# Order of heads in the small matmuls of a recurrent branch, halves of a product, and a stacked low-rank pass

## The chip, the cores and the metric

The kernel runs on one core of one Trainium2 chip. The metric is the device time of one execution in microseconds; the median of three runs stands for the kernel.

## What is computed

One layer of a hybrid model over 2048 positions and 1024 channels, in float32: an input projection, a gated MLP branch with a spatial product in chunks of 128, a recurrent branch of eight heads, a gated merge of both, an output projection with residual and layer norm, and a feed-forward layer of 4096 with residual and layer norm. The change touches the recurrent branch:

```python
r, k, v, xw, xa, xg = jnp.split(z, [i1, i2, i3, i4, i5], axis=-1)
w_log = -jax.nn.softplus(-(w0 + jnp.tanh(xw) @ w_decay_up)) - 0.5
decay = jnp.exp(-jnp.exp(w_log.astype(jnp.float32)))
a = jax.nn.sigmoid(a0 + xa @ w_aaa_up)
...
def step(state, inp):
    rt, wt, kt, vt, at, bt = inp
    sa = jnp.einsum('bhij,bhj->bhi', state, at)
    state = (state * wt[:, :, None, :] + sa[..., None] * bt[:, :, None, :]
             + vt[..., None] * kt[:, :, None, :])
    yt = jnp.einsum('bhij,bhj->bhi', state, rt)
    return state, yt
```

The two products with `w_decay_up` and `w_aaa_up` contract over 32 values each; they are called the low-rank products below. Heads have 64 channels.

## The kernel before

The sequence is cut into four blocks of 512 positions. The large products (projections, gates, merge, output, feed-forward) are run as three float32r matmuls each, on a high and a low part of both operands (`mm3`, lines 453 to 455), with 512 columns. Weights come from DRAM as tiles of 128 x 1024 (`wraw`); ScalarE casts the high part `whi` (line 387), VectorE subtracts to the low part `wlo` (line 388), one tile ahead of their use.

The recurrent branch is computed in chunks of 64 positions. A block has four half-blocks of 128 positions (two chunks), and the eight heads are four pairs; of a pair the even head lies in partitions 0 to 63 (`half[0]`, `E`), the odd one in 64 to 127 (`half[1]`, `O`). Each half-block passes three stages, all in plain f32:

- `rwkv_a`, for each pair: the low-rank products into `ua` (lines 587, 588), decays and scaled operands on ScalarE and VectorE, then the score products `s0` and `s1` (line 625; even head on the upper rows of the array, odd head on the lower), a sum over a head (626) and transposes (628). The operand `xwa` is computed per block in `proj_rwkv`, goes out to DRAM (`xd`) and comes back per half-block, into two sets of buffers.
- `rwkv_b`: the inverse of a triangular matrix per head and chunk. VectorE makes the 32 x 32 diagonal blocks in 31 steps (lines 687, 688), they pass through DRAM (`td`, `TT`), are transposed on VectorE into `T11` (line 708), and 32 x 32 matmuls make the off-diagonal block (lines 712 and 719), first all of the even heads, then all of the odd ones.
- `rwkv_c`, for each of two chunks: Q's product `xy` (line 759) of the state with the chunk's operands, with all 128 weights columns of `G`, so that one product gives both the value that the inverse is applied to (copied to `Xs`) and the first part of the output; the product with the inverse, `TT` (line 768); the state update (774); the second part of the output, added in place (780). Each runs over the four pairs of the even heads, then over those of the odd ones. Copies out of PSUM are split between VectorE and ScalarE by head.

TensorE's instructions stand in the order in which the program is written; the other engines' order is chosen by a scheduler when the program is built. The large products are generators that yield after every two k-tiles (six matmuls), and `weave` takes a step of the recurrent branch whenever the step before has had its number of yields (`Y_C` is 2, `Y_T` 12, and so on). So between two small groups lies a fixed number of large matmuls. Block 0's recurrent branch runs beside the projections of blocks 0 and 1, that of each later block beside the feed-forward and projections around it. The very first products (`first`, from `first_tiles` in `setup`) run before any of this.

Of the kernel before, what the change touches and what calls it, by code (L numbers as in the profile page):

```python
# [16 lines left out]
P = 128  # L17
# [3 lines left out]
TB = 512  # L21
# [68 lines left out]
class Body:  # L90
# [122 lines left out]
    def setup(self):  # L213
# [69 lines left out]
        self.lora = const.tile([C, 2, RW], F32, name="lora")  # L283
        nc.sync.dma_start(out=self.lora, in_=A["lora"])
# [226 lines left out]
    def proj_rwkv(self, b):  # L511
        nc, A = self.nc, self.A
        if self.h_of != b:
            self.go(self.load_h(b))
        xwa = self.work.tile([C, TB], F32, name="xwa", tag="t2", bufs=3)
        pp = self.pre[0] if b == 0 else (yield from self.fm(self.hT, m=C))
        self.shift_mix(pp, C, "xwa", 0, 12, xwa)
        nc.scalar.activation(xwa[0:32], xwa[0:32], AF.Tanh)
        xg = self.work.tile([96, TB], F32, name="xg", tag="t2", bufs=3)
        pp = self.pre[1] if b == 0 else (yield from self.fm(self.hT, m=96))  # L520
        self.shift_mix(pp, 96, "xg", 0, 13, xg)
        nc.scalar.activation(xg, xg, AF.Tanh, scale=0.5)
        nc.vector.tensor_scalar(xg, xg, 0.5, 0.5, op0=ALU.mult, op1=ALU.add)
        xd = self.dr.tile([TB // HB, C + 96, HB], F32, name="xd", tag="xd", bufs=2)
        nc.sync.dma_start(out=xd[:, 0:C].rearrange("h p t -> p h t"), in_=xwa.rearrange("p (h t) -> p h t", t=HB))
        nc.sync.dma_start(out=xd[:, C:].rearrange("h p t -> p h t"), in_=xg.rearrange("p (h t) -> p h t", t=HB))
        zd = [self.dr.tile([TB // HB, P, 3, HB], F32, name=f"zd{p}", tag=f"zd{p}", bufs=2) for p in range(NP)]
        self.spill["z", b] = (xd, zd)
# [25 lines left out]
    def rwkv_a(self, b, h, q):  # L554
# [13 lines left out]
        xd, zd = self.spill["z", b]  # L568
        xwa = rp.tile([C, HB], F32, name="xwa", tag="xwa", bufs=2)
        nc.sync.dma_start(out=xwa, in_=xd[h, 0:C])  # L570
        xg = rp.tile([96, HB], F32, name="xg", tag="xg", bufs=2)
        nc.sync.dma_start(out=xg, in_=xd[h, C:])
# [8 lines left out]
        def first(p):  # L581
# [5 lines left out]
            nc.tensor.matmul(ua[:, 0], lhsT=self.lora[:, 0, fs], rhs=xwa, start=True, stop=True)  # L587
            nc.tensor.matmul(ua[:, 1], lhsT=self.lora[:, 1, fs], rhs=xwa, start=True, stop=True)
# [31 lines left out]
        def second(p, bk, kp):  # L620
            zr, zk, zv = (zq[:, p, j] for j in range(3))
            s0, s1 = pst([P, 3, P], "s0"), pst([P, 4, P], "s1")
            for i, sc in enumerate((s0, s1)):
                for c in range(NC):
                    nc.tensor.matmul(sc[:, c], lhsT=bk[half[i], c], rhs=G[i][half[i], p, c], start=True, stop=True)  # L625
# [38 lines left out]
    def rwkv_b(self, q):  # L664
# [52 lines left out]
        for i, (lo, hi) in enumerate(qd):  # L717
            for u in range(U16):
                nc.tensor.matmul(tps[lo, u], lhsT=Zs[hi, u], rhs=TT[hi, u, 32:64], start=True, stop=True)
# [5 lines left out]
    def rwkv_c(self, b, h, q):  # L725
# [20 lines left out]
        for c in range(NC):  # L746
# [14 lines left out]
            Xs = rp.tile([P, NP, C], F32, name="Xs", tag="Xs", bufs=1)  # L761
            nc.vector.tensor_copy(out=Xs[E], in_=xy[E, 0])
            nc.scalar.copy(out=Xs[O], in_=xy[O, 1])
            yield Y_C
            for i in range(2):
                r = half[i]
                for p in range(NP):
# [4 lines left out]
            for i in range(2):  # L772
                for p in range(NP):
# [4 lines left out]
            for i in range(2):  # L778
                for p in range(NP):
                    nc.tensor.matmul(xy[half[1 - i], i, p], lhsT=AB[half[i], p, c, cr[i]:cr[i] + C], rhs=Q[half[i], i, p],  # L780
                                     start=False, stop=True, skip_group_check=True)
            nc.vector.tensor_mul(self.Sc[self.scur], St, PC[:, c][:, :, None].to_broadcast([P, NP, C]))
            nc.scalar.copy(out=Yt[half[c], :, 0], in_=xy[O, 0])
            nc.vector.tensor_copy(out=Yt[half[c], :, 1], in_=xy[E, 1])
# [303 lines left out]
def arrange(np, inp):  # L1088
# [37 lines left out]
    lora = np.zeros((64, 2, 512), w.dtype)  # L1126
    lora[:32, 0] = inp["w_decay_up"][0]
    lora[32:, 1] = inp["w_aaa_up"][0]
    a["lora"] = lora
# [44 lines left out]
```

## Time and profile before

| | |
|---|---|
| median of 3 runs | 3103.5 us (3100.29 to 3109.51) |
| the profiled execution | 3111.15 us |
| its span, first to last instruction | 3109.3 us |
| TensorE busy | 3046.7 us (98%) |
| VectorE busy | 2124.0 us (68%) |
| ScalarE busy | 1263.4 us (41%) |

The page of the profile gives busy times over the whole span. Matmuls are pipelined, so they overlap in the records, and how long a stretch of TensorE takes is read from the starts in the timeline. In the timeline, equal instructions that follow each other stand in one row with their count, and the time of the row goes from the first start to the last end. A f32 matmul leaves two matmul records, a float32r one leaves one. PE is TensorE, DVE is VectorE, ACT is ScalarE.

### The profile page before, as it was taken

The page shows a single profiled execution, that of the slowest core. Times are in us where ns is not written, and L with a number is a line of the kernel's source. Part 1 is how long each engine was busy: PE and PEld are TensorE (multiplying, and loading weights), DVE is VectorE, ACT ScalarE, POOL GpSimd, SP SyncE. Part 2 cuts the span into 40 slices and gives each one's busy share as a digit, 9 for nine tenths or more (in the row PEclk, how much of TensorE's full clock was granted, in tenths as well). Part 3 has the DMA queues.
Part 4 walks back from the last instruction along what each step waited for, and adds up shares of the span by engine and source line. Part 5 has one row for each costly group of instructions (what it writes and reads, how often), then busy time and mean ns, then how long its engine had stood idle before and what let it go on. Part 6 is the DMA issues. An engine that isn't in the chain of part 4 may idle for free.

```text
span 3109.3 us, 44483 instructions
## 1 busy us (share of the span) xinstructions
PE 3046.7 (98%) x16432; PEld 2455.4 (79%) x16432; DVE 2124.0 (68%) x4727; ACT 1263.4 (41%) x2012; POOL 149.2 (5%) x370
## 2 busy tenths in 40 slices
PE   8999999999999999999999999999999999999998
PEld 6776878777777877878787888787878888888887
DVE  7877874778777686486777657567668755854446
ACT  5534433353343334444433343453444334253332
POOL 1101100000000000100000000110000000000000
PEclk9999999999999999999999999999999999999999
DMA  8565544832323265433323246534333224622332
GB/s 286 158 177 165 169 135 161 271 102 86 98 82 102 82 204 190 152 129 120 104 92 93 89 142 205 164 121 148 118 97 93 84 95 146 223 88 95 98 99 95
DMA packets 241483, 416.71 MB, mean 134 GB/s; under 512 B 72465, under 2 KB 127377, under 8 KB 241265
## 3 DMA queue, kind: packets, MB, share of 16 engines
q1 hardware_dynamic: 241184, 413.59, 41.7%
q8 instruction: 130, 2.13, 0.3%
q14 instruction: 89, 0.72, 0.1%
q0 software_dynamic: 80, 0.26, 0.0%
HBM read 357.60 MB, written 56.17 MB: 133 GB/s over the span
## 4 chain that ended last, share of the span: by engine, by line
PE 85%; DVE 9%; DMA 4%; issue 1%; ACT 1%; SPq 0%; POOL 0%; DVEq 0%; ACTq 0%
PE fm_ps L453 15%; PE fm_ps L455 14%; PE fm_ps L454 14%; PE ff L453 7%; PE ff L454 7%; PE ff L455 7%; PE xy L759 2%; DVE wlo L388 1%; PE ops L454 1%; PE ops L455 1%; PE ops L453 1%; DVE tmp L687 1%; PE s L625 1%; PE vps L453 1%; PE us L768 1%
## 5 line engine op out<-in xcount | busy, mean ns | idle before, releaser
L387 ACT CAST whi<-wraw 128x1024 fp32r<-128x1024 f32 (+1 forms) x500 | 495.0, 991 | 880.7 <-PE fm_ps L454 439.5
L388 DVE TENSOR_TENSOR wlo<-wraw,whi 128x1024 fp32r<-128x1024 f32 (+1 forms) x500 | 573.0, 1148 | 343.2 <-ACT whi L387 335.7
L453 PE MATMUL fm_ps<-xh,whi 128*128 128x512 f32 x1984 | 796.1, 401 | 3.6 <-ACT xh L387 2.2
L454 PE MATMUL fm_ps<-xl,whi 128*128 128x512 f32 x1984 | 774.4, 390 | 2.8 <-DVE xl L388 2.8
L455 PE MATMUL fm_ps<-xh,wlo 128*128 128x512 f32 x1984 | 775.7, 391 | 0.6 <-DVE wlo L388 0.6
L453 PEld LDWEIGHTS fm_ps<-xh,whi 128*128 128x128 f32 x1984 | 370.8, 187 | 91.9 <-issue 5.2
L455 PEld LDWEIGHTS fm_ps<-xh,wlo 128*128 128x128 f32 x1984 | 370.8, 187 | 84.0 <-DVE wlo L388 1.5
L454 PEld LDWEIGHTS fm_ps<-xl,whi 128*128 128x128 f32 x1984 | 371.4, 187 | 77.4 <-DVE xl L388 4.3
L453 PE MATMUL ff<-hh,whi 128*128 128x512 f32 (+1 forms) x1056 | 416.2, 394 | 1.9 <-DVE zr L1051 1.2
L454 PE MATMUL ff<-hl,whi 128*128 128x512 f32 (+1 forms) x1056 | 404.8, 383 | 0.3 <-DVE hl L388 0.3
L455 PE MATMUL ff<-hh,wlo 128*128 128x512 f32 (+1 forms) x1056 | 405.1, 384 | 0.0
L1051 DVE SCALAR_TENSOR_TENSOR zr<-ff,mod,zr 128x512 f32<-128x512 f32 (+1 forms) x264 | 184.9, 730 | 138.6 <-PE ff L455 138.1
L453 PEld LDWEIGHTS ff<-hh,whi 128*128 128x128 f32 x1056 | 198.6, 188 | 46.2 <-issue 6.0
L455 PEld LDWEIGHTS ff<-hh,wlo 128*128 128x128 f32 x1056 | 198.4, 188 | 40.3
L454 PEld LDWEIGHTS ff<-hl,whi 128*128 128x128 f32 x1056 | 198.8, 188 | 35.6 <-DVE hl L388 0.5
L687 DVE TENSOR_TENSOR tmp<-T,L 128x4 f32<-128x4 f32 (+23 forms) x496 | 162.3, 327 | 10.2
L688 DVE TENSOR_REDUCE T<-tmp 128x1 f32<-128x4 f32 (+23 forms) x496 | 122.9, 248 | 10.5
L388 DVE TENSOR_TENSOR hl<-r,hh 128x512 fp32r<-128x512 f32 x128 | 87.7, 688 | 47.8 <-ACT hh L387 47.3
L454 PE MATMUL ops<-wlo,mh 128*128 128x512 f32 x256 | 103.0, 402 | 5.4 <-DVE wlo L388 5.4
L453 PE MATMUL ops<-whi,mh 128*128 128x512 f32 x256 | 102.8, 402 | 1.7 <-DVE ga L914 1.7
L453 PE MATMUL fm_ps<-yh,whi 128*128 128x512 f32 x256 | 102.2, 399 | 1.7 <-ACT yh L387 1.2
L455 PE MATMUL fm_ps<-yh,wlo 128*128 128x512 f32 x256 | 101.5, 397 | 2.0 <-DVE wlo L388 2.0
(236 smaller groups left out, 4018.9 us busy)
## 6 DMA issues: line engine op xcount, KB each, us to landing
wraw<-in_w_ff_dram SPq DMA_DIRECT2D x260, 512.0 KB
wraw<-in_w_gate_dram SPq DMA_DIRECT2D x64, 512.0 KB
wada<-in_w_ada_dram SPq DMA_DIRECT2D x48, 512.0 KB
wraw<-in_w_rkv_dram SPq DMA_DIRECT2D x42, 512.0 KB
gd<-g SPq DMA_DIRECT2D x64, 256.0 KB
ga<-gd SPq DMA_DIRECT2D x64, 256.0 KB
wraw<-in_w_out_dram SPq DMA_DIRECT2D x32, 512.0 KB
zd<-zmix SPq DMA_DIRECT2D x48, 256.0 KB
```

The source lines that it names most:

```text
L387: nc.scalar.copy(out=hi, in_=src)
L388: nc.vector.tensor_sub(lo, src, hi.bitcast(F32))
L453: nc.tensor.matmul(ps, lhsT=wh, rhs=xh, start=start, stop=False)
L454: nc.tensor.matmul(ps, lhsT=wh, rhs=xl, start=False, stop=False)
L455: nc.tensor.matmul(ps, lhsT=wl, rhs=xh, start=False, stop=stop)
L625: nc.tensor.matmul(sc[:, c], lhsT=bk[half[i], c], rhs=G[i][half[i], p, c], start=True, stop=True)
L687: nc.vector.tensor_mul(tmp[:, :n, :w], T[:, :n, :w], L[:, :w, t][:, None, :].to_broadcast([P, n, w]))
L688: nc.vector.tensor_reduce(T[:, :n, t:t + 1], tmp[:, :n, :w], axis=AX.X, op=ALU.add)
L759: nc.tensor.matmul(xy[:, i, p], lhsT=G[i][:, p, c], rhs=Q[:, i, p], start=(i == 0 and p == 0), stop=False, skip_group_check=True)
L768: nc.tensor.matmul(us[r, 0, p], lhsT=TT[r, p * NC + c], rhs=Xs[r, p], start=True, stop=True)
L1051: self.nc.vector.scalar_tensor_tensor(res[:, n, ts], pfs[i], self.mod[:, 40 + n:41 + n], res[:, n, ts], op0=ALU.mult, op1=ALU.add)
```

## The change

Four things change.

- In `rwkv_a` (scores), `rwkv_b` (both 32 x 32 products) and `rwkv_c` (all products) the loops change places: the even and the odd head of a pair follow each other, then comes the next pair or chunk.
- Q's product is split: the 64 columns that give the value for the inverse go to the free half of `us`, the other 64 to `xy`, which is now half the size. `Xs` is copied in one operation on VectorE.
- The low-rank products are done in float32r in one pass over 128 rows. In `lora` rows 0 to 63 hold the rounded weights twice (32 rows each) and rows 64 to 127 hold, twice, what the rounding left; in `xwa` the high and the low part of its 32 values stand in turn, twice. So one product sums the four products of parts.
- So `setup` casts `lora` on ScalarE, subtracts on VectorE and casts again; `proj_rwkv` splits `xwa` per block and stores both parts (`xs`); `rwkv_a` loads them with four DMAs in place of one, into one set of buffers in place of two.

```diff
-        self.lora = const.tile([C, 2, RW], F32, name="lora")
-        nc.sync.dma_start(out=self.lora, in_=A["lora"])
+        self.lora = const.tile([P, 2, RW], F32R, name="lora")
+        lr = self.sp.tile([P, 2, RW], F32, name="lraw", tag="lraw")
+        for i in range(4):
+            nc.sync.dma_start(out=lr[i * 32:i * 32 + 32], in_=A["lora"])
+        nc.scalar.copy(out=self.lora, in_=lr)
+        nc.vector.tensor_sub(lr[C:], lr[C:], self.lora[C:].bitcast(F32))
+        nc.scalar.copy(out=self.lora[C:], in_=lr[C:])
...
+        parts = [self.work.tile([C, TB], F32R, name=f"xwa{n}", tag="t2", bufs=3) for n in range(2)]
+        self.split(xwa, *parts)
+        for n in range(2):
+            nc.sync.dma_start(out=xs[:, n].rearrange("h p t -> p h t"), in_=parts[n].bitcast(F32).rearrange("p (h t) -> p h t", t=HB))
...
-        xwa = rp.tile([C, HB], F32, name="xwa", tag="xwa", bufs=2)
-        nc.sync.dma_start(out=xwa, in_=xd[h, 0:C])
+        xwa = rp.tile([P, 2, HB], F32R, name="xwa", tag="xwa", bufs=1)
+        for i in range(4):
+            nc.sync.dma_start(out=xwa[i * 32:i * 32 + 32].bitcast(F32),
+                              in_=xs[h, i % 2].rearrange("(a p) t -> p a t", a=2))
...
-            nc.tensor.matmul(ua[:, 0], lhsT=self.lora[:, 0, fs], rhs=xwa, start=True, stop=True)
-            nc.tensor.matmul(ua[:, 1], lhsT=self.lora[:, 1, fs], rhs=xwa, start=True, stop=True)
+            for i in range(2):
+                nc.tensor.matmul(ua[:, i], lhsT=self.lora[:, i, fs], rhs=xwa[:, i], start=True, stop=True)
...
-            for i, sc in enumerate((s0, s1)):
-                for c in range(NC):
+            for c in range(NC):
+                for i, sc in enumerate((s0, s1)):
...
-        for i, (lo, hi) in enumerate(qd):
-            for u in range(U16):
+        for u in range(U16):
+            for i, (lo, hi) in enumerate(qd):
                 nc.tensor.matmul(zps[hi, u], lhsT=AB[lo, u // NC, u % NC, ca[i] + 32:ca[i] + 64], rhs=T11[lo, u],
                                  start=True, stop=True)
...
-            xy = pst([P, 2, NP, C], "xy")
+            xy = pst([P, NP, C], "xy")
             us = pst([P, 2, NP, C], "us")
-            for i in range(2):
-                for p in range(NP):
-                    nc.tensor.matmul(xy[:, i, p], lhsT=G[i][:, p, c], rhs=Q[:, i, p], start=(i == 0 and p == 0),
+            for p in range(NP):
+                for i in range(2):
+                    nc.tensor.matmul(us[half[i], 1, p], lhsT=G[i][:, p, c, half[i]], rhs=Q[:, i, p], start=True, stop=True)
+            Xs = rp.tile([P, NP, C], F32, name="Xs", tag="Xs", bufs=1)
+            nc.vector.tensor_copy(out=Xs, in_=us[:, 1])
+            for p in range(NP):
+                for i in range(2):
+                    nc.tensor.matmul(xy[half[1 - i], p], lhsT=G[i][:, p, c, half[1 - i]], rhs=Q[:, i, p], start=p == 0,
                                      stop=False, skip_group_check=True)
...
-            for i in range(2):
-                r = half[i]
-                for p in range(NP):
+            for p in range(NP):
+                for i in range(2):
+                    r = half[i]
                     nc.tensor.matmul(us[r, 0, p], lhsT=TT[r, p * NC + c], rhs=Xs[r, p], start=True, stop=True)
```

TensorE, first chunk of the first half-block in stage C: `Q` is the right operand, `G_625` and `G_626` hold the even and the odd heads' weights, and the `fm_ps` rows are large matmuls of the projections. Before:

```order
L455 MATMUL fm_ps<-xh_149,wlo 128x512
L759 MATMUL xy<-Q,G_625 128x64 x4
L759 MATMUL xy<-Q,G_626 128x64 x4
L453 MATMUL fm_ps<-xh_150,whi 128x512
L454 MATMUL fm_ps<-xl_158,whi 128x512
```

The same place now, where `G_638` and `G_639` are the even and the odd heads' weights:

```order
L461 MATMUL fm_ps<-xh_149,wlo 128x512
L772 MATMUL us<-Q,G_638 64x64
L772 MATMUL us<-Q,G_639 64x64
...
L777 MATMUL xy<-Q,G_638 64x64
L777 MATMUL xy<-Q,G_639 64x64
...
L459 MATMUL fm_ps<-xh_150,whi 128x512
```

Eight matmuls with outputs of 128 partitions have become sixteen with outputs of 64, in pairs of an even and an odd head, at the same place between the large ones.

ScalarE, behind the first products: `zraw` and the `mix` operations read the results of `first`, and `whi` are the first weight tiles of the projections. Before:

```order
L387 CAST xh_155<-ht 128x512
L387 CAST whi<-wraw 128x1024 x2
L506 ACTIVATE zraw<-first_164,vecs 64x512
L508 ACTIVATE xwa<-first_164,mix 64x512
L506 ACTIVATE zraw<-first_165,vecs 96x512
L508 ACTIVATE xg<-first_165,mix 96x512
L518 ACTIVATE xwa<-xwa 32x512
L506 ACTIVATE zraw<-first_166,vecs 128x512
```

Now:

```order
L512 ACTIVATE zraw<-first_164,vecs 64x512
L514 ACTIVATE xwa<-first_164,mix 64x512
L288 CAST lora<-lraw 128x1024
L524 ACTIVATE xwa<-xwa 32x512
L512 ACTIVATE zraw<-first_165,vecs 96x512
L514 ACTIVATE xg<-first_165,mix 96x512
L290 CAST lora<-lraw 64x1024
L528 ACTIVATE xg<-xg 96x512
L393 CAST xwa_558<-xwa 64x512
L512 ACTIVATE zraw<-first_166,vecs 128x512
L512 ACTIVATE zraw<-first_167,vecs 128x512
L393 CAST whi<-wraw 128x1024 x3
```

The first casts of weight tiles stood ahead of the operations on the first products and now stand behind eleven operations.

## Rows read from the trace of the kernel before

**Rows 1.** The page, part 1: busy us, share of the span, records.
```profile
PE 3046.7 (98%) x16432; PEld 2455.4 (79%) x16432; DVE 2124.0 (68%) x4727; ACT 1263.4 (41%) x2012; POOL 149.2 (5%) x370
```

**Rows 2.** Timeline of TensorE, a low-rank pair: start us, us, instruction, count.
```profile
67.71 0.39 PE L455 MATMUL fm_ps<-xh,wlo 128*128 128x512 f32 x1
68.03 0.48 PE L587 MATMUL ua<-xwa,lora 64*128 64x128 f32 x2
...
68.67 0.50 PE L453 MATMUL fm_ps<-xh,whi 128*128 128x512 f32 x1
69.00 0.39 PE L454 MATMUL fm_ps<-xl,whi 128*128 128x512 f32 x1
```

**Rows 3.** Timeline of TensorE, last feed-forward: float32r with 256 columns.
```profile
3080.06 0.28 PE L455 MATMUL ff<-hh,wlo 128*128 128x256 f32 x1
3080.18 0.28 PE L453 MATMUL ff<-hh,whi 128*128 128x256 f32 x1
```

**Rows 4.** Timeline of TensorE, Q's product.
```profile
206.77 0.39 PE L455 MATMUL fm_ps<-xh,wlo 128*128 128x512 f32 x1
207.00 1.89 PE L759 MATMUL xy<-Q,G 128*128 128x64 f32 x16
208.70 0.48 PE L453 MATMUL fm_ps<-xh,whi 128*128 128x512 f32 x1
```

**Rows 5.** Timeline of TensorE, the product with the inverse.
```profile
211.63 0.96 PE L768 MATMUL us<-Xs,TT 64*64 64x64 f32 x16
212.52 0.50 PE L453 MATMUL fm_ps<-xh,whi 128*128 128x512 f32 x1
```

**Rows 6.** By form; then three timelines of 0.01 us: what is in flight.
```profile
L768 PE MATMUL us<-Xs,TT 64*64 64x64 f32 x512 | 30.8, 224 | 0.0
...
211.63 0.44 PE L768 MATMUL us<-Xs,TT 64*64 64x64 f32 x4
...
211.92 0.44 PE L768 MATMUL us<-Xs,TT 64*64 64x64 f32 x7
...
212.20 0.33 PE L768 MATMUL us<-Xs,TT 64*64 64x64 f32 x3
```

**Rows 7.** Timeline of TensorE, state update.
```profile
215.48 0.97 PE L774 MATMUL us<-Q,BK 128*64 128x64 f32 x16
```

**Rows 8.** Timelines of TensorE, 32 x 32 pieces: the group, 0.01 us inside it.
```profile
201.27 1.09 PE L719 MATMUL tps<-TT,Zs 32*32 32x32 f32 x32
...
201.57 0.38 PE L719 MATMUL tps<-TT,Zs 32*32 32x32 f32 x10
```

**Rows 9.** Timelines of TensorE: score products twice, and the spatial product.
```profile
79.28 1.39 PE L625 MATMUL s<-G,bk 64*128 64x128 f32 x8
...
95.73 0.72 PE L625 MATMUL s<-G,bk 64*128 64x128 f32 x8
...
450.25 1.09 PE L864 MATMUL sp<-wsT,v 128*64 128x128 f32 x16
```

**Rows 10.** Timelines of ScalarE and TensorE behind the first products.
```profile
50.35 1.99 ACT L387 CAST whi<-wraw 128x1024 fp32r<-128x1024 f32 x2
56.48 0.69 ACT L506 ACTIVATE zraw<-first,vecs 64x512 f32<-64x512 f32 x1 [4.13 <-PE first L455]
57.06 0.76 ACT L508 ACTIVATE xwa<-first,mix 64x512 f32<-64x512 f32 x1
...
61.14 0.39 PE L453 MATMUL fm_ps<-xh,whi 128*128 128x512 f32 x1
```

**Rows 11.** A window (us, then busy us and records of PE, PEld, DVE, ...); timeline, all engines.
```profile
740.00:781.00 41.00, 41.00 (x197) 32.04 (x196) 40.00 (x125) 15.46 (x28) 1.50 (x6) 1.00 0.23 72
...
787.26 0.43 DVE L708 STREAM_TRANSPOSE T<-TT 32x256 f32<-32x256 f32 x1 [4.20 <-DMA TT<-td]
...
787.74 0.69 PE L712 MATMUL zps<-T,AB 32*32 32x32 f32 x16 [0.91 <-DVE T L708]
```

**Rows 12.** A window: as above; the number behind POOL is the granted clock.
```profile
1196.50:1203.00 6.50, 5.15 (x12) 4.10 (x13) 6.50 (x11) 2.04 (x4) 0.00 (x0) 0.56 0.68 218
```

More of the change, by code (lines that the diff above doesn't have):

```diff
@@ L523, in proj_rwkv @@
         nc.vector.tensor_scalar(xg, xg, 0.5, 0.5, op0=ALU.mult, op1=ALU.add)
-        xd = self.dr.tile([TB // HB, C + 96, HB], F32, name="xd", tag="xd", bufs=2)
-        nc.sync.dma_start(out=xd[:, 0:C].rearrange("h p t -> p h t"), in_=xwa.rearrange("p (h t) -> p h t", t=HB))
-        nc.sync.dma_start(out=xd[:, C:].rearrange("h p t -> p h t"), in_=xg.rearrange("p (h t) -> p h t", t=HB))
+        xd = self.dr.tile([TB // HB, 96, HB], F32, name="xd", tag="xd", bufs=2)
+        xs = self.dr.tile([TB // HB, 2, C, HB], F32, name="xs", tag="xs", bufs=2)
+        parts = [self.work.tile([C, TB], F32R, name=f"xwa{n}", tag="t2", bufs=3) for n in range(2)]
+        self.split(xwa, *parts)
+        for n in range(2):
+            nc.sync.dma_start(out=xs[:, n].rearrange("h p t -> p h t"), in_=parts[n].bitcast(F32).rearrange("p (h t) -> p h t", t=HB))
+        nc.sync.dma_start(out=xd.rearrange("h p t -> p h t"), in_=xg.rearrange("p (h t) -> p h t", t=HB))
         zd = [self.dr.tile([TB // HB, P, 3, HB], F32, name=f"zd{p}", tag=f"zd{p}", bufs=2) for p in range(NP)]
-        self.spill["z", b] = (xd, zd)
+        self.spill["z", b] = (xd, xs, zd)
         for p in range(NP):
@@ L567, in rwkv_a @@
             yield Y_Z
-        xd, zd = self.spill["z", b]
-        xwa = rp.tile([C, HB], F32, name="xwa", tag="xwa", bufs=2)
-        nc.sync.dma_start(out=xwa, in_=xd[h, 0:C])
+        xd, xs, zd = self.spill["z", b]
+        xwa = rp.tile([P, 2, HB], F32R, name="xwa", tag="xwa", bufs=1)
+        for i in range(4):
+            nc.sync.dma_start(out=xwa[i * 32:i * 32 + 32].bitcast(F32),
+                              in_=xs[h, i % 2].rearrange("(a p) t -> p a t", a=2))
         xg = rp.tile([96, HB], F32, name="xg", tag="xg", bufs=2)
-        nc.sync.dma_start(out=xg, in_=xd[h, C:])
+        nc.sync.dma_start(out=xg, in_=xd[h])
         zq = rp.tile([P, NP, 3, HB], F32, name="zq", tag="zq", bufs=2)
@@ L716, in rwkv_b @@
         yield Y_V2
-        for i, (lo, hi) in enumerate(qd):
-            for u in range(U16):
+        for u in range(U16):
+            for i, (lo, hi) in enumerate(qd):
                 nc.tensor.matmul(tps[lo, u], lhsT=Zs[hi, u], rhs=TT[hi, u, 32:64], start=True, stop=True)
@@ L754, in rwkv_c @@
             yield Y_C
-            xy = pst([P, 2, NP, C], "xy")
+            xy = pst([P, NP, C], "xy")
             us = pst([P, 2, NP, C], "us")
-            for i in range(2):
-                for p in range(NP):
-                    nc.tensor.matmul(xy[:, i, p], lhsT=G[i][:, p, c], rhs=Q[:, i, p], start=(i == 0 and p == 0),
+            for p in range(NP):
[6 more added lines that the diff above has]
+                    nc.tensor.matmul(xy[half[1 - i], p], lhsT=G[i][:, p, c, half[1 - i]], rhs=Q[:, i, p], start=p == 0,
                                      stop=False, skip_group_check=True)
-            Xs = rp.tile([P, NP, C], F32, name="Xs", tag="Xs", bufs=1)
-            nc.vector.tensor_copy(out=Xs[E], in_=xy[E, 0])
-            nc.scalar.copy(out=Xs[O], in_=xy[O, 1])
             yield Y_C
-            for i in range(2):
-                r = half[i]
-                for p in range(NP):
+            for p in range(NP):
+                for i in range(2):
+                    r = half[i]
                     nc.tensor.matmul(us[r, 0, p], lhsT=TT[r, p * NC + c], rhs=Xs[r, p], start=True, stop=True)
@@ L771, in rwkv_c @@
             yield Y_C
-            for i in range(2):
-                for p in range(NP):
+            for p in range(NP):
+                for i in range(2):
                     nc.tensor.matmul(us[half[i], 1, p], lhsT=BK[:, p, c, half[i]], rhs=Q[:, i, p], start=True, stop=True)
@@ L777, in rwkv_c @@
             self.scur ^= 1
-            for i in range(2):
-                for p in range(NP):
-                    nc.tensor.matmul(xy[half[1 - i], i, p], lhsT=AB[half[i], p, c, cr[i]:cr[i] + C], rhs=Q[half[i], i, p],
+            for p in range(NP):
+                for i in range(2):
+                    nc.tensor.matmul(xy[half[1 - i], p], lhsT=AB[half[i], p, c, cr[i]:cr[i] + C], rhs=Q[half[i], i, p],
                                      start=False, stop=True, skip_group_check=True)
             nc.vector.tensor_mul(self.Sc[self.scur], St, PC[:, c][:, :, None].to_broadcast([P, NP, C]))
-            nc.scalar.copy(out=Yt[half[c], :, 0], in_=xy[O, 0])
-            nc.vector.tensor_copy(out=Yt[half[c], :, 1], in_=xy[E, 1])
+            nc.scalar.copy(out=Yt[half[c], :, 0], in_=xy[O])
+            nc.vector.tensor_copy(out=Yt[half[c], :, 1], in_=xy[E])
         yv = Yt.rearrange("p k h i -> p (k h) i")
@@ L1125, in arrange @@
     a["b_spatial"] = inp["b_spatial"][0]
[L1126 to L1129, printed above, removed]
+    a["lora"] = np.stack([inp["w_decay_up"][0], inp["w_aaa_up"][0]], axis=1)
     a["c"] = inp["c"][0]
```

## The prediction

> **What bounds the kernel now.** I read the page first. TensorE is busy 3046.7 of 3109.3 us, VectorE 68%, ScalarE 41% [rows 1], so what matters is how long the TensorE queue takes to pass, not what the other engines do. Then I read the timeline of TensorE alone around each kind of small matmul and took distances from start to start, since the ends are modelled. A record is one matmul line of the profile; a f32 matmul of the program leaves two, a float32r one leaves one. The usual neighbours, float32r with 512 columns, start 0.23 us apart, as does what stands behind one of them in [rows 4]. A small group costs what it adds to that step. It has three parts: an entry (0.32 in place of 0.23 when the group uses part of the array's rows or columns [rows 2], none when it uses the whole array [rows 4]), a body, and a slower first big matmul behind it (0.33 [rows 2]). None of the lines shown carries an idle time, except in [rows 11].
>
> **The change part by part.** All sums are against the profiled execution, 3111.15 us (span 3109.3 and 1.85 around it). It is 7.65 above the median of the runs, 3103.5, and I carry the difference over to the median.
>
> *Low-rank products.* Now: from the last big matmul at 67.71 to the second one after at 69.00 is 1.29 us for two steps worth 0.46, so the pair costs 0.83 [rows 2]. After: two float32r records that use the whole array, so no entry and no slow neighbour. Their 128 columns by 128 weights are not in this trace. Nearest is float32r with 256 columns: 0.12 apart [rows 3]. From 0.23 at 512 to 0.12 at 256 the columns alone would give 0.07 at 128, but whole-array f32 groups with only 64 columns do not go below 0.11 (sixteen records in 1.70 [rows 4]), so the weights set a floor there. I take 0.12. The other end is the f32 duration kept, 0.23. Saved: 0.83 - 0.24 = 0.59, times 64 pairs (4 blocks, 4 half-blocks, 4 head pairs): **37.8 us**. Bounds: 0.07 each gives 44, 0.23 each gives 24.
>
> *The halves that alternate.* The question is whether two matmuls in different parts of the array run side by side. Three places say yes. The score products (one half of the rows, then the other) pass in 0.72 from first start to last end where the second half was ready, and in 1.39 where it had to wait [rows 9]. The spatial matmuls already alternate column halves: sixteen records with 128 columns in 1.09 [rows 9], while a 64-column record of the whole array already takes 0.11. And in line 768, where the even heads end and the odd ones begin, seven records fit into 0.44 us, where at the front four did [rows 6]. With a record's length of 0.22 a half alone steps by (0.33 - 0.22) / 2 = 0.058, after a first step of 0.107 [rows 6]. The second half starts 0.287 in, when the first has four records left, so only that stretch overlaps today. Alternating, it all does: 0.107 + 6 x 0.058 + 0.006 + 0.148 (the way out, which is what 0.89 leaves today [rows 5]) = 0.61 in place of 0.89. Line 768 saves 0.28 x 32 = **9.0**. Line 774's sixteen records take as long (0.97 [rows 7] to 0.96 [rows 5]), and line 780's have the form of line 768's: **18.0**.
>
> Lines 712 and 719 are the same with 32 x 32 pieces: 32 records in 1.09 [rows 8], and as in [rows 5] the next matmul begins 0.07 before the last of them ends. With the same overlap of four records that is 0.032 a step; alternating, 0.05 + 14 x 0.032 + 0.12 = 0.62 in place of 1.02, over 32 groups **12.8**. The score products overlap already: nothing.
>
> *Q's product.* Now sixteen records in 1.70, no entry, a slow neighbour of 0.33: 1.80 [rows 4]. After, 32 records of half the weights, in 16 side-by-side pairs in one stretch: entry 0.09 more, 0.107 + 14 x 0.058 + 0.006 + 0.148 = 1.07, slow neighbour 0.10 more: 1.27. Saved 0.53, over 32 groups **17.0**. If the halves did not overlap, the body would be 0.107 + 30 x 0.058 + 0.15 = 2.0 and this edit would lose 12. The single copy to Xs on VectorE replaces one on each engine with the same 256 columns. It has two generator steps (12 big matmuls, 2.7 us) as cover, and is released earlier than now.
>
> Gross: 37.8 + 9.0 + 18.0 + 12.8 + 17.0 = **94.6 us**.
>
> *What is added.* (a) At the start. ScalarE casts the first two weight tiles at 50.35 today, before the first projection ends at 56.48 [rows 10]. In the new order the first of them stands behind eleven operations that cannot begin before 56.48: four biases (0.58 each), two mixes (0.67), two tanh and the cast of xwa (about 0.53), two casts of lora (1.0): 7.3 us, so the cast ends near 64.8. TensorE wants it at 61.14 [rows 10]. That is 3.6 of idle time, and 0.7 more for the low part, which VectorE forms behind it. The low part of xwa then goes through DRAM later too; the first low-rank product may wait 1 us. I take 5, from 0 (if the releases come otherwise) to 9. (b) The inverse. In the first half-block of block 1 VectorE is busy 40.00 of 41 us, and line 712 then waits 0.91 for the transpose behind it, which itself waits 4.20 for a DMA [rows 11]. There is no slack there, so the 2.4 us that four low-rank pairs save just ahead come back as waiting. The first half-block of block 0 is alike. I take 5 for both, and 1 for the rest. Alternation also puts the wait of the odd half one matmul behind the even one: where they become ready apart (sixteen of the 32 stand alone at 787.74 [rows 11]) the group gains nothing; 1. (c) The clock. In the 6.5 us around the end of one of today's longest waits the granted clock averages 0.56 of 2.4 GHz, so most of them pass at 1.2, and twelve big matmuls took 5.15 us, for which 0.23 each would be 2.8 [rows 12]. A new wait of that kind costs 2 to 3 us more than itself; I take one, at 3. (d) Three more DMA issues per half-block and one set of buffers for xwa instead of two: SP waits for the last low-rank product of the half-block before, with weight loads queued behind it. Next use is a whole C stage or 20 us later; nothing. Together 5 + 7 + 3 = **15**.
>
> Net 94.6 - 15 = 80: 3031 for an execution like the profiled one, **3024** against the median.
>
> *Two rules weighed.* In [rows 6] both halves write one PSUM bank and step together. The Trainium skill (TensorEngine Tiling, Gotcha 1: PSUM Pressure) says that different row tiles cannot access one PSUM bank at the same time. By that rule lines 768, 780, 712 and 719 would gain nothing; it is the third rival, and the trace speaks against it. In [rows 8] ten records of 0.19 lie within 0.38, a mean step of 0.021. The Trainium skill (TensorE: Matmul & The Clock Gate, "Wait — 56ns, not 53.3ns?") gives about 25 ns as the least distance of two starts; by it lines 712 and 719 would save 0.1 a group, 10 less in all, and this trace goes below it for ten records at least.
>
> **The rivals.**
> 1. *Float32r with 128 columns is no quicker than 512.* 2 x 0.23 a pair costs 14 more: 3038. For: no row of that shape. Against: 256 columns take half of 512 [rows 3].
> 2. *A steady pace limits short records.* The overlaps of short records seen so far last three or four pairs; what feeds the array might not keep that up over 32. At 0.032 a record, the steady pace of [rows 8], lines 712 and 719 save nothing (12.8), the 96 groups of lines 768, 774 and 780 0.05 less each (4.8), Q 0.1 less (3.2): 21 more, 3045.
> 3. *One bank, one half.* 9.0 + 9.0 + 12.8 go: 3055. Against: [rows 6].
> 4. *VectorE becomes the bound in blocks 0 and 1.* A half-block saves 94.6 / 16 = 5.9; if all eight there give it back, 47 go in place of 6: 3065. For: [rows 11]. Against: the waits there are short today.
> 5. *Slower: every change of half is paid like an entry.* 0.09 each, with no overlap, over some 1600 changes: 146 lost, and the loss of today's overlap (23 + 4) and Q's 12 eat the 38 of the low-rank part: about 3265. Without overlap any price decides. Against: line 864, whose fifteen changes all lie within 1.09 [rows 9].
>
> **How the numbers follow.** Forecast 0.62 (its own range 3006 to 3040), rivals 0.12, 0.10, 0.04, 0.07, 0.03, the first two together 0.02 (3058). The upper end takes in rivals 1 and 2 with a few us of waits; the lower is the gross sum with 44 for the low-rank part and hardly a new wait: 3004 to 3052. About 0.3% (9 us) is what a measurement can tell from no change. Faster 0.95; same 0.02; slower 0.03.
>
> **What would show it.** The low-rank pair: 0.24 between big neighbours and no slow one after. Line 768's group 0.61 from first start to next big one; 712's and 719's 0.62; Q's 1.07. An idle TensorE of 3 to 5 us near 61, and longer waits for line 708 near 195 and 780. It is wrong if the alternating groups keep 0.89, or if waits of TensorE for VectorE grow by more than 20 us.

## The result and the profile after

The changed kernel takes 3051.26 us (median of four runs, 3046.05 to 3053.34), the kernel before 3104.38 beside it: a ratio of 0.9826, 95% interval 0.9806 to 0.9845. That is 53 us faster where 80 were forecast, inside the range of 3004 to 3052 but at its upper end. The profiled execution took 3053.34 us, 57.8 less than that of before. The first part of the page, which answers [rows 1]:

```profile
PE 2966.9 (97%) x16816; PEld 2381.7 (78%) x16816; DVE 2121.5 (70%) x4732; ACT 1253.8 (41%) x1986; POOL 150.8 (5%) x370
```

TensorE is still the busy engine, at 97% in place of 98%. Span less busy time is its idle time: 84.7 us, before 62.6. The timeline of TensorE alone (start, us, instruction, count) shows each small group between its large neighbours. First a low-rank pair, which answers [rows 2]:

```profile
150.31 0.40 PE L461 MATMUL fm_ps<-xh,wlo 128*128 128x512 f32 x1
150.54 0.33 PE L600 MATMUL ua<-xwa,lora 128*128 128x128 f32 x2
150.71 0.44 PE L459 MATMUL fm_ps<-xh,whi 128*128 128x512 f32 x1
151.00 0.39 PE L460 MATMUL fm_ps<-xl,whi 128*128 128x512 f32 x1
```

From 150.31 to 151.00 is 0.69 us for two steps worth 0.46: the pair costs 0.23. Then Q's product in two parts, the product with the inverse, state update and second part of the output, which answer [rows 4, 5, 7]:

```profile
213.82 0.39 PE L461 MATMUL fm_ps<-xh,wlo 128*128 128x512 f32 x1
214.13 0.69 PE L772 MATMUL us<-Q,G 128*64 128x64 f32 x16
214.65 0.64 PE L777 MATMUL xy<-Q,G 128*64 128x64 f32 x16
215.22 0.50 PE L459 MATMUL fm_ps<-xh,whi 128*128 128x512 f32 x1
...
218.16 0.68 PE L783 MATMUL us<-Xs,TT 64*64 64x64 f32 x16
218.77 0.50 PE L459 MATMUL fm_ps<-xh,whi 128*128 128x512 f32 x1
...
221.72 0.69 PE L789 MATMUL us<-Q,BK 128*64 128x64 f32 x16
222.34 0.68 PE L795 MATMUL xy<-Q,AB 64*64 64x64 f32 x16
222.95 0.50 PE L459 MATMUL fm_ps<-xh,whi 128*128 128x512 f32 x1
```

And a group of 32 x 32 pieces, which answers [rows 8]:

```profile
208.72 0.69 PE L731 MATMUL tps<-TT,Zs 32*32 32x32 f32 x32
209.34 0.50 PE L459 MATMUL fm_ps<-xh,whi 128*128 128x512 f32 x1
```

Sixteen records of 64 x 64 now take 0.61 from first start to next big matmul, 32 of 32 x 32 take 0.62, Q's 32 take 1.09. Taken as the median over all groups of a kind, the savings are 0.61 a low-rank pair, 0.51 for Q, 0.28 for the product with the inverse, 0.56 for the two behind it, 0.40 for each group of 32 x 32. Over all groups that is 95.0 us, where the prediction had 94.6. So the records came out as forecast, and 37 us went elsewhere in the profiled pair, where 15 were forecast.

Both kernels run the same 11520 large matmuls in the same order, so the time between two of them can be compared stretch by stretch. The table gives, from the starts in the traces, what each stretch lost or saved against before, and what the small groups in it save by their records alone:

| stretch (large matmuls) | before, us | saved | by records | lost |
|---|---|---|---|---|
| start (to 240) | 59.6 | -7.0 | 0.6 | 7.6 |
| block 0's branch (240 to 1560) | 412.9 | 8.3 | 20.0 | 11.8 |
| its end, merge, output (1560 to 2600) | 277.0 | 10.2 | 8.0 | -2.2 |
| block 1's branch (2600 to 3700) | 330.8 | 8.3 | 18.9 | 10.6 |
| blocks 2 and 3 (3700 to 9600) | 1582.5 | 37.9 | 47.5 | 9.6 |

Both sides come from one profiled execution, and that of before lies 7 us above its kernel's median. The waits of TensorE (waiting line, releaser, total us, times, longest) say where. Three new or grown ones of block 0's branch in the changed kernel:

```profile
PE s L637 <- DVE bk L627: 4.9, 5, 3.0
PE yp L815 <- DVE Yt L810: 3.0, 1, 3.0
...
PE s L637 <- DVE T L700: 2.0, 1, 2.0
```

The score products, L637, are of stage A and do not stand among the long waits of this stretch before. The wait of L815 is for the output at the end of stage C; before it was 0.3.

Four windows of block 0's branch in the changed kernel (us, then busy us and records of PE, PEld, DVE, ACT, POOL, then clock):

```profile
228.00:246.00 18.00, 18.00 (x119) 14.44 (x118) 11.43 (x37) 4.62 (x7) 0.00 (x0) 1.00 0.85 104
...
318.00:336.00 18.00, 18.00 (x171) 14.14 (x171) 11.26 (x24) 7.66 (x11) 2.38 (x6) 1.00 0.58 181
...
352.00:373.00 21.00, 18.76 (x90) 15.13 (x89) 20.59 (x59) 11.06 (x23) 4.89 (x7) 1.00 0.68 208
373.00:390.00 17.00, 15.99 (x71) 12.88 (x72) 16.23 (x50) 6.56 (x14) 3.44 (x11) 0.80 0.47 129
```

The last two hold low-rank pairs and scores of stage A; VectorE is busy 98 and 95% there, and TensorE waits, above all once, 2.96 us for `bk` across the border of the two. The first two hold products of stage C; VectorE is busy 63% in both, and TensorE does not wait. These windows are the clear cases: over the eight half-blocks of blocks 0 and 1 VectorE was busy 70 to 97% in stage A before the change and 32 to 88% in stage C. What each stage saved is read from sums over eight windows each, of stage A (first low-rank pair to last scores) before and now, and of stage C (behind the inverse to the second part of the output) before and now:

```profile
sum 354.00, PE 344.70 PEld 267.11 DVE 301.92 ACT 178.32 POOL 35.93; mean PE 43.09 PEld 33.39 DVE 37.74 ACT 22.29 POOL 4.49
...
sum 346.80, PE 328.05 PEld 258.70 DVE 303.06 ACT 178.18 POOL 38.13; mean PE 41.01 PEld 32.34 DVE 37.88 ACT 22.27 POOL 4.77
...
sum 273.20, PE 273.20 PEld 220.81 DVE 176.25 ACT 95.06 POOL 8.40; mean PE 34.15 PEld 27.60 DVE 22.03 ACT 11.88 POOL 1.05
...
sum 250.20, PE 249.27 PEld 192.12 DVE 173.31 ACT 89.75 POOL 11.97; mean PE 31.16 PEld 24.02 DVE 21.66 ACT 11.22 POOL 1.50
```

Stage A, with VectorE busy 85% on average, became 7.2 us shorter where its 32 pairs save 19.5, and TensorE's idle time in it doubled from 9.3 to 18.8. Stage C, with VectorE busy 65%, became 23.0 shorter where its groups save 21.6. The share alone does not decide, though: in stage A of blocks 2 and 3 VectorE was busy 73 to 91%, and there 17.5 of the same 19.5 came through.

### The profile page after: what moved, and what is told of

Same layout as the page of the kernel before. It is cut to its first block, busy times and chain, and to the rows that moved or that the text cites. A ratio compares the mean times of both kernels' runs of the same rounds, so it can differ in the third digit from the quotient of the medians.

```text
span 3051.6 us, 45340 instructions
## 1 busy us (share of the span) xinstructions
PE 2966.9 (97%) x16816; PEld 2381.7 (78%) x16816; DVE 2121.5 (70%) x4732; ACT 1253.8 (41%) x1986; POOL 150.8 (5%) x370
## 4 chain that ended last, share of the span: by engine, by line
PE 74%; DVE 16%; DMA 5%; ACT 3%; issue 2%; POOL 0%; SPq 0%; DVEq 0%; ACTq 0%; POOLq 0%
PE fm_ps L459 13%; PE fm_ps L460 13%; PE fm_ps L461 13%; PE ff L459 6%; PE ff L460 6%; PE ff L461 6%; DVE wlo L394 3%; DVE tmp L699 2%; DVE T L700 2%; PE ops L460 1%; PE ops L461 1%; PE ops L459 1%; PE s L637 1%; PE vps L459 1%; PE vps L461 1%
## 5 line engine op out<-in xcount | busy, mean ns | idle before, releaser
L699 DVE TENSOR_TENSOR tmp<-T,L 128x4 f32<-128x4 f32 (+23 forms) x496 | 162.3, 327 | 10.3
```

The source lines that it names most:

```text
L699: nc.vector.tensor_mul(tmp[:, :n, :w], T[:, :n, :w], L[:, :w, t][:, None, :].to_broadcast([P, n, w]))
```

## The experiments

The theory at first: the small groups save what their records show, and the rest is lost at the start and where VectorE is full, in blocks 0 and 1. The rivals: a part of the change makes its own waits (the low-rank path by its way through DRAM, the copy to Xs, the alternation), or the start alone.

**One part at a time.** Three kernels, each with one part of the change on the kernel before. The first:

```diff
-            nc.tensor.matmul(ua[:, 0], lhsT=self.lora[:, 0, fs], rhs=xwa, start=True, stop=True)
-            nc.tensor.matmul(ua[:, 1], lhsT=self.lora[:, 1, fs], rhs=xwa, start=True, stop=True)
+            for i in range(2):
+                nc.tensor.matmul(ua[:, i], lhsT=self.lora[:, i, fs], rhs=xwa[:, i], start=True, stop=True)
```

> Only the low-rank products are changed (float32r, stacked; both splits, their DMAs and the new start), all loops and Q stay as before. In the changed kernel a pair costs 0.23 in place of 0.84, so 64 pairs give 39 us, and the start there costs 7.7. Theory (the missing gain is lost where VectorE is full, in blocks 0 and 1, by whichever part saves time there): 39 - 7.7 - about 9 of waits, 3082 us. Rival (the low-rank path itself, with its way through DRAM and one set of buffers, makes the waits): nearly all of the 37 lost is lost here, 3095 to 3103.

3093.57 us, ratio 0.9956 (0.9944 to 0.9969): 12 us gained of 39. By stretches: 8.1 lost at the start, 8.3 in block 0's branch (0.9 saved of 9.1), 1.3 behind it, 5.6 in block 1's branch (0.8 slower than before, where 4.9 were due), and nothing in blocks 2 and 3 (21.2 of 19.5). The theory's 3082 is missed by 12, and the time lies close to the rival's 3095. But blocks 2 and 3 have the same way through DRAM and the same one set of buffers and lose nothing, which speaks against the rival's cause.

The second has the loops exchanged (scores, both 32 x 32 products, the last three of stage C), Q whole:

```diff
-            for i in range(2):
-                r = half[i]
-                for p in range(NP):
+            for p in range(NP):
+                for i in range(2):
+                    r = half[i]
```

> Only the order of heads is changed (scores, both 32 x 32 products, the product with the inverse, state update, second part of the output); Q's product is whole and in the old order, the low-rank products are plain f32. Groups cost 0.28, 0.56 and 0.40 less: 9 + 18 + 12.8 = 39.8 us. Theory (waits where VectorE is full): about 8 of it lost, 3072 us. If the groups alone decide: 3064. If the order itself makes the waits (the odd half waits behind the even one): 25 lost, 3089.

3072.04 us, 0.9893 (0.9879 to 0.9906): 33.5 gained of 39.8, as the theory had it. Of 7.8 due in block 0's branch 6.4 came, of 9.9 in block 1's 5.7. The 25 us that the order itself might have cost are not there.

The third splits Q's product:

```diff
-                    nc.tensor.matmul(xy[:, i, p], lhsT=G[i][:, p, c], rhs=Q[:, i, p], start=(i == 0 and p == 0),
+                    nc.tensor.matmul(us[half[i], 1, p], lhsT=G[i][:, p, c, half[i]], rhs=Q[:, i, p], start=True, stop=True)
```

> Only Q's product is split in column halves, with the one copy to Xs on VectorE; the other loops and the low-rank products as before. A group costs 1.28 in place of 1.79: 16.4 us. Theory: 3 to 4 lost in waits for VectorE, 3091 us. Rival (the copy to Xs, now wholly on VectorE, holds up the product with the inverse or fills VectorE further): 3098 or more.

3086.75 us, 0.9939 (0.9927 to 0.9952): 18.8 gained, more than the 13 of the theory and a little more than the 16.4 of the records, so the single copy to Xs on VectorE costs nothing that shows. Both other parts give what they should; only the low-rank part falls short. The three gains add to 64 us, and all three together give 53.

**VectorE relieved.** The inverse's steps on VectorE are stopped half way, once on the kernel before, once with the low-rank part alone. Both kernels leave out the rest of the diagonal blocks.

```diff
-        for t in range(1, 32):
+        for t in range(1, 16):
...
-            if t % 4 == 3:
+            if t % 2 == 1:
```

> The kernel before with the inverse's VectorE steps stopped half way (t to 15 in place of 31, as many yields; what they would have filled of T is left out), which takes some 13 us of VectorE off each half-block and nothing off TensorE. Of 48 us of waits in the kernel before about 10 fall where VectorE is full (blocks 0 and 1): 3094 us. It is the yardstick for the next run.

> The run with only the low-rank products changed, with the same shortening of the inverse as in the run before it. Theory (in stage A of blocks 0 and 1 VectorE sets the pace, so what TensorE saves there comes back as waiting): with VectorE relieved the 39 us of the pairs come through but for the 8 at the start, 28 to 31 us under the shortened kernel before, where the same change gave 12. Rival (the waits come from the low-rank path itself, its DMAs, its one set of buffers or the late start alone): 12 to 15 us under it.

3091.95 and 3066.75 us: with VectorE relieved the low-rank part gives 25 us in place of 12, somewhat under the 28 of the theory and far from the rival's 15. In the profiled executions alone it is 24 in place of 18, because the profiled one of before was a long one. The stretches say what is left: the start still loses 10, block 0's branch gives 3.6 of 9.1 (0.9 without the relief), block 1's 4.7 of 4.9. TensorE's waits in block 1's branch with the low-rank part alone are these; in the same stretch of the relieved kernel the view has no row:

```profile
PE ff L459 <- DVE zr L1063: 2.5, 1, 2.5
PE zps L724 <- DVE T L720: 2.3, 2, 1.7
PE tps L731 <- issue: 1.0, 1, 1.0
PE s L638 <- DVE kp L629: 0.7, 1, 0.7
PE fm_ps L459 <- DVE zr L1063: 0.3, 1, 0.3
```

In this stretch of the kernel before stand 1.2 for `zr`, 1.3 for `T` and 0.7 for `kp`. So the pairs' saving in block 1 is lost to VectorE. It is lost mostly behind stage A, at the inverse (`T`) and at the feed-forward, which waits for the residual addition on VectorE (`zr`). In block 0 this pair of runs shows it for a part only.

**VectorE's work moved away.** No work is left out here: 16 products of the modulation (1.2 us of VectorE each) are put behind block 0.

```diff
-M1 = 24
+M1 = 8
...
-Y_M3 = 3
+Y_M3 = 2
```

> The changed kernel with 16 of the modulation products (1.2 us of VectorE each, 20 us) moved from block 0 to the merge and output projection behind it; no work is left out. Theory (VectorE sets the pace in block 0): half of the 12 us of waits there go, and little comes where they go to, where VectorE is busy three quarters of the time: 3045 us. Rival (VectorE's total does not matter, only its order or the start): 3051 or more.

3065.58 us, 14 slower than the changed kernel. In block 0's branch the theory holds: 18.8 of 20.0 us come through in place of 8.3. The window that answers the third of those above:

```profile
352.00:373.00 21.00, 21.00 (x103) 16.92 (x101) 19.72 (x57) 11.63 (x24) 4.21 (x12) 1.00 0.61 178
```

VectorE is at 94% and TensorE no longer waits. Two things weaken the reading. A high share alone holds nothing up: in the run with Q split alone VectorE is busy 98% near the same place, and TensorE waits nowhere:

```profile
345.00:366.00 21.00, 21.00 (x102) 16.59 (x102) 20.66 (x63) 11.51 (x23) 2.66 (x7) 1.00 0.54 170
```

And the start loses 10.3 here in place of 7.6, and a later start gives something back in block 0 by itself, as the first run on the start below shows. The weight tiles that move along with the products are no rival in block 0: TensorE waits 0.4 for weights in its branch in the changed kernel.

But the merge and output projection, which got the products, lose 22 us. TensorE's waits there, from 600 to 640:

```profile
PE ops L460 <- DVE wlo L394: 6.3, 3, 4.6
PE ops L459 <- ACT whi L393: 2.7, 2, 1.4
```

The products' tiles (`wada`) take turns with the weights in three buffers, so the weights come late; that a VectorE at 74% (95.86 of 129.60 us before) had room was the wrong question. Whether the buffers or VectorE held the weights up was not separated.

**The start.** Three tries to mend it on the changed kernel. In the first the first weight tile is fetched behind the first products' loop:

```diff
         self.pre = [ps[:m] for ps, m in zip(pss, ms)]
+        w = next(self.todo)
+        self.ahead.append((w[1], self.fetch(*w)))
```

> The changed kernel with the first weight tile fetched and cast at the end of the first products, ahead of the casts of lora and the operations on the first results. Theory: the 3.65 us of idle time near 60, the 0.8 behind it and the 1.4 of lower clock go, the wait of 1.3 for xwa stays: 5 to 6 us less than the changed kernel, 3045 us. Rival (block 0 is paced by VectorE, so an earlier start comes back as waiting in it): 3051.

3052.94 us, no change. The start now loses 12.8 in place of 7.6, and block 0's branch 7.8 in place of 11.8, though no work of VectorE was moved. The wait for the weights near 60, here in TensorE's timeline of the changed kernel

```profile
64.10 0.80 PE L459 MATMUL fm_ps<-xh,whi 128*128 128x512 f32 x1 [3.65 <-ACT whi L393]
...
75.22 0.41 PE L600 MATMUL ua<-xwa,lora 128*128 128x128 f32 x2 [1.32 <-DMA xwa<-xs]
```

is gone, and in the timeline of the mended one two others stand behind it:

```profile
68.99 0.50 PE L461 MATMUL fm_ps<-xh,whi 128*128 128x512 f32 x1 [2.69 <-ACT zmix L516]
78.09 0.66 PE L602 MATMUL ua<-xwa,lora 128*128 128x128 f32 x2 [6.89 <-DMA xwa<-xs]
```

On VectorE the low part of xwa now came behind two subtractions for weights, and its loads stood behind stores of zmix on SP's queue. The second try puts lora's and xwa's split on GpSimd, with its queue for xwa:

```diff
-        nc.scalar.copy(out=self.lora, in_=lr)
-        nc.vector.tensor_sub(lr[C:], lr[C:], self.lora[C:].bitcast(F32))
+        nc.gpsimd.tensor_copy(out=self.lora, in_=lr)
+        nc.gpsimd.tensor_sub(lr[C:], lr[C:], self.lora[C:].bitcast(F32))
...
-            nc.sync.dma_start(out=xs[:, n]
+            nc.gpsimd.dma_start(out=xs[:, n]
```

> The changed kernel with the start mended wholly: lora's casts and subtraction and the low part of xwa on GpSimd, the stores and loads of both parts of xwa on GpSimd's queue, the first weight tile fetched before the last k-step of the first products. Theory: no idle time near 60, low-rank product without a wait of over 1 us near 70, so 7 us are gained by the end of the start; what VectorE holds back in block 0 decides how much of it lasts: 3044 to 3048 us. Rival (the start is not the cause of block 0's loss, all comes back): 3051. If GpSimd's work slows VectorE: above 3055.

3058.23 us, 0.985 (0.9835 to 0.9864), 7 us above the changed kernel, whose interval it still touches: the wait for xwa is 4.78, that for zmix 3.15. The third keeps the split on ScalarE and VectorE, writes the low part over xwa, so that it takes one buffer less of the three that zmix shares, and uses GpSimd's queue for the DMAs alone:

```diff
-        parts = [self.work.tile([C, TB], F32R, name=f"xwa{n}", tag="t2", bufs=3) for n in range(2)]
+        parts = [self.work.tile([C, TB], F32R, name="xwah", tag="t2", bufs=3), xwa.bitcast(F32R)]
```

> The changed kernel with the start mended again: first weight tile fetched ahead of the first results' operations; the low part of xwa written over xwa itself, so that the split takes one buffer of the three that zmix shares in place of two; stores and loads of both parts on GpSimd's queue, with no computation there. Theory: no idle time near 60, the wait for zmix near 66 and the 4 to 7 us of the first low-rank product for xwa go too, so the 7.7 us lost at the start come back, and VectorE gives some of it back in block 0: 3044 to 3048 us. Rival (block 0 is paced by VectorE from the first pair on, and all comes back): 3051.

3049.22 us, 0.9826 (0.9809 to 0.9843): no difference that can be told. The weights' wait is gone, xwa's is 1.2 as in the changed kernel, and that for zmix is left (ScalarE's row first, then TensorE's):

```profile
67.44 1.45 ACT L516 ACTIVATE zmix<-first,mix 128x512 f32<-128x512 f32 x2 [2.74 <-DMA xs<-xwah]
...
68.94 0.50 PE L461 MATMUL fm_ps<-xh,whi 128*128 128x512 f32 x1 [2.35 <-ACT zmix L516]
```

ScalarE's zmix waits 2.74 there for the store of the high part, which still holds one of the three buffers. The start loses 6.4 in place of 7.6, and block 0's branch 8.8 in place of 11.8. So the expectation failed by its first half: the start was never mended. The idle time near 60 was only the first of three waits in line.

**Half a microsecond off VectorE.** Two small operations of stage A go to ScalarE, alone and with the third start.

```diff
-            nc.vector.tensor_scalar(sg, sg, 1.0, None, op0=ALU.add)
+            nc.scalar.activation(sg, sg, AF.Identity, bias=self.one)
...
-            nc.vector.tensor_scalar(kp, at, self.ka_h[:, p:p + 1], self.ka_c[:, p:p + 1], op0=ALU.mult, op1=ALU.add)
+            nc.scalar.activation(kp, at, AF.Identity, scale=self.ka_h[:, p:p + 1], bias=self.ka_c[:, p:p + 1])
```

> The changed kernel with two small operations of stage A (adding 1 to sg, 0.21 us, and forming kp from at, 0.33 us) on ScalarE in place of VectorE: 0.54 us of VectorE for each of 64 pairs, 2.2 us a half-block, about what the low-rank pairs save TensorE there (2.4). Nothing is left out. Theory (VectorE's share of stage A sets the pace in blocks 0 and 1): a third to a half of the 20 us lost in blocks 0 and 1 comes back, 3041 to 3045 us. Rival (it is the chain of single operations or ScalarE's queue of casts that sets the pace): 3051 or more.

> Both of the edits of the two runs before it, on the changed kernel. If they act in different places: the sum of their gains, 3034 to 3041 us. If both only move the same wait: not below the better of the two.

3051.74 and 3052.23 us: nothing. Block 0's branch loses 14.2 with it in place of 11.8, block 1's 8.0 in place of 10.6. The Trainium skill (Perfetto Trace Analysis, Optimizing Scalar/DVE Operations) says that moving some work off a saturated VectorE to ScalarE may make sense; here it did not. The waits show the work come back in other places; the changed kernel first, then this one:

```profile
PE s L637 <- DVE bk L627: 4.9, 5, 3.0
PE zps L724 <- DVE T L720: 2.8, 4, 1.7
...
PE zps L726 <- DVE T L722: 7.7, 4, 3.2
PE s L639 <- DVE bk L629: 2.9, 5, 0.6
PE sp L881 <- ACT u L875: 2.8, 1, 2.8
PE s L639 <- ACT at L606: 2.1, 1, 2.1
```

The scores wait less for VectorE's `bk`, but now for ScalarE's `at`; the spatial product waits for ScalarE's `u`, and the inverse longer for `T`. What the other runs show is that 13 us a half-block (the shortened inverse) were enough in block 1 and 5 (the moved products) in block 0; that the 13 were not enough in block 0 is not explained.

**Low-rank products new only where VectorE has room.** Blocks 0 and 1 keep the old pair and its one load:

```diff
+                if b < 2:
+                    nc.tensor.matmul(ua[:, i], lhsT=self.lora[:, i, fs], rhs=xwa,
+                                     start=True, stop=True)
+                else:
+                    nc.tensor.matmul(ua[:, i], lhsT=self.lora[:, i, fs], rhs=xwa[:, i], start=True, stop=True)
```

> The changed kernel with the old low-rank products (plain f32, no split of xwa, one load) in blocks 0 and 1 and the new ones in blocks 2 and 3 alone; lora is loaded, and in blocks 2 and 3 split, once per block. TensorE has 32 pairs of 0.84 in place of 0.23 back: 19.5 us more records than the changed kernel. Theory (in blocks 0 and 1 TensorE is held by VectorE's part of the recurrent branch within a fixed number of large matmuls, so the saving of the pairs there does not reach the end, and their start costs 7.7): those 19.5 are more than covered, by some 7 at the start and some 20 of waits in blocks 0 and 1, and it comes to 3038 to 3045 us, faster than the changed kernel. Rival (each part's gain adds, the pairs of blocks 0 and 1 bring 19.5 less 7.7 for the start): 3063 us.

3047.15 us, 0.9811 (0.9796 to 0.9825). With 19.5 us more of records on TensorE it is no slower than the changed kernel. The rival, 3063, is out; of the theory's gain of 6 to 13 only some 4 are seen, which the intervals cannot tell from none. By stretches nothing is lost at the start (0.3 saved) and in block 0's branch (10.7 of 10.9); block 1's loses 4.1 in place of 10.6, blocks 2 and 3 lose 8.9, as before. So the 32 new pairs of blocks 0 and 1 bring nothing that shows in the changed kernel.

Blocks 2 and 3 lose 9 with all parts together, when each part alone gives there what its records do (21.2, 22.8 and 10.1 us). About 5 of it are waits of TensorE (15.6 in place of 10.5). Two groups of them stand neither there before nor with the low-rank part alone, an operand of the feed-forward and the `kp` of stage A:

```profile
PE pf L459 <- DVE xh L391: 2.0, 2, 1.0
PE s L638 <- DVE kp L629: 1.5, 2, 0.7
```

So VectorE holds something back there too. How much is not sure: the first run on the start and the one with the moved products change nothing in blocks 2 and 3 and lose 4.0 and 12.7 there, so one execution's 9 can be off by several us.

## Why the prediction was right, and where it was off

*The terms of the records.* All held: 0.23 for the low-rank pair (0.24), 0.61 and 0.62 for the alternating groups (0.61, 0.62), 1.28 for Q's (1.27). The bounds were hardly needed. Rivals 1 (float32r at 128 columns no quicker), 2 (a steady pace), 3 (one bank) and 5 (a price for each change of half) fall by these rows, and neither of the two rules weighed shows in them. One reading was wrong without harm: the sixteen records of line 864 are eight matmuls, so they hold seven changes of half and not fifteen.

*Start, step (a).* ScalarE's order was read rightly: 3.65 of idle time, where 3.6 were forecast. The step's 5 us of waits came (3.65 for the weights, 0.2 for their low part, 1.3 for xwa). The start lost 7.6, because the large matmuls behind the wait, from 64.7 to 69, stand 0.43 apart at half the clock (granted 0.51), which costs 2.6; that belongs to step (c).

*The inverse, step (b).* Here the prediction was off. It took 7 us for waits: 5 for the first half-blocks of blocks 0 and 1, where [rows 11] showed a wait, 1 for all others, whose waits were short before, and 1 for the alternation. TensorE's idle time grew by 22.1, so by 17 outside the start: 8.1 in block 0's branch, 5.3 in block 1's, 5.1 in blocks 2 and 3, less 1.3 between. A wait of zero before was taken for room on VectorE. The sums by stage show in its place that of 19.5 us which the pairs save in stage A of blocks 0 and 1 only 7.2 come through there. The window of [rows 11], with VectorE busy 40.00 of 41 us, is not every stage A; the eight were at 70 to 97%. Rival 4 had this mechanism, and priced it with the whole saving of a half-block (5.9), stage C's too. That was too much: stage C kept its savings. With the clock's share in it, 20 are lost from block 0's branch to block 1's (11.8 - 2.2 + 10.6), between the forecast's 7 and rival 4's 47, and some 10 more in blocks 2 and 3. By the prediction's own sign of being wrong, waits for VectorE that grow by more than 20, it was not: they grew from 26.5 to 42.4, by 16.

*The clock, step (c).* One stretch at the lower clock was forecast, at 3 us. Leaving out the end of the span, where TensorE stands still, the kernel before has six such stretches (granted 0.50 to 0.51) and the changed one thirteen, and TensorE is busy in them for 31.7 and 50.2 us. With large matmuls 0.43 apart in place of 0.23, somewhat under half of that is the clock's price: 9 us more, an estimate from these rows, 2.6 of it at the start. In block 1's branch there was none before, and there are 10 us now, each stretch near one of the longer waits (777 and 930).

*The DMAs, step (d).* Held: the only wait of TensorE for xwa in the changed kernel is the 1.3 at the start, and taking its DMAs off SP's queue changed nothing that shows.

So 15 was forecast for what is added, 12 of waits and 3 of clock, and 37 is what the profiled pair shows: 22 of waits, about 9 of clock and 6 that are not accounted for. That VectorE is the cause of the waits is shown by its relief in block 1, in part in block 0, and only by the releasers named in the view in blocks 2 and 3. That the range held was luck: its upper end was made from rivals 1 and 2, which did not happen, and not from rival 4, which in part did.

## What to carry to other kernels

Ask of every saving in which stage it lies, and how busy the next engine is in that stage: a wait of zero on the busy engine does not say that the other has room. In blocks 0 and 1 VectorE, busy 85% in stage A and 65% in stage C, let 7.2 of 19.5 us through in the first and all in the second. A busy share alone does not decide it (98% passed without a wait in one run), so take the share as a place to look and the waits and starts as the answer. Count the lower clock behind each new wait as well. Where work is moved to the head of a queue, look at the second and third wait behind the one that goes. When a part of a change pays in some blocks only, make it there alone: the new low-rank pairs of blocks 0 and 1, with their split, loads and start, could be left out at no loss.

## What the runs showed of the hardware

Products of 64 x 64 in the upper and the lower rows of the array, all with results in one tile of PSUM, pass as fast alternating as products whose results are in different column halves: 0.61 (L783) and 0.62 (L789). The Trainium skill (TensorEngine Tiling, Gotcha 1: PSUM Pressure) says that different row tiles cannot access the same PSUM bank at once; by that the alternation of L783 would have gained nothing, and the measurement shows otherwise.

GpSimd's work seems able to hold VectorE up. In the second try at the start a mix operation on VectorE (96 x 512) took 2.64 us while GpSimd subtracted (timelines of GpSimd and of VectorE); the same operation took 0.75 in the third try, where GpSimd did not compute (last row):

```profile
57.24 2.72 POOL L334 TENSOR_TENSOR lraw<-lraw,lora 64x1024 f32<-64x1024 f32 x1
...
57.87 2.64 DVE L522 SCALAR_TENSOR_TENSOR xg<-zraw,vecs,xg 96x512 f32<-96x512 f32 x1 [0.17 <-ACT xg L521]
...
59.02 0.75 DVE L517 SCALAR_TENSOR_TENSOR xg<-zraw,vecs,xg 96x512 f32<-96x512 f32 x1 [0.49 <-ACT xg L516]
```

The first two end at 59.96 and 60.51. It is one case. The Trainium skill (GPSIMD Engine Reference, 1. Specifications) has GpSimd's way to SBUF shared with VectorE, and this pair of rows agrees.
